# Sampled-token attention in a hybrid decoder layer: cached keys turned together and scored in one visit, cached values in two steps, new tokens' products paired

## The chip, the cores and the metric

The kernel runs on one core of a Trainium2 chip. The metric is device time in microseconds for one execution of the whole layer; lower is better. Three runs of the kernel before took 1364.67, 1366.31 and 1366.91 us, a median of 1366.31.

The engines are named as in the profile: PE (TensorE, matrix products; PEld is its loading of the stationary operand), DVE (VectorE), ACT (ScalarE), POOL (GpSimd) and SP (SyncE, which here only issues DMAs). ACT issues some DMAs as well. Each engine works through its own list in order and waits for others by semaphores.

## The reference, cut to what matters

One layer runs over a prompt (1024 tokens) and over a sample (8 sequences of 4 new tokens, each with cached keys and values). The change touches the sample's dilated attention:

```python
def dilated_attn_cached(q, k, v, buf, d, span):
    # q, k, v: (8, 4, 4 heads, 128); buf: (8, Wb, 2, 4, 128), Wb = 128, 256, 256 for the groups
    kall = concatenate([buf[:, :, 0], k], axis=1)
    vall = concatenate([buf[:, :, 1], v], axis=1)
    idx = Wb + arange(T)[:, None] - arange(span + 1)[None, :] * d
    kg, vg = take(kall, maximum(idx, 0), axis=1), take(vall, maximum(idx, 0), axis=1)
    s = einsum('bthe,btjhe->bthj', q, kg) / sqrt(128)
    s = where(idx >= 0, s, -1e30)
    m = max(s); p = exp(s - m); l = sum(p)
    return einsum('bthj,btjhe->bthe', p, vg) / l, m + log(l)
...
wts = softmax(stack(lses), axis=0)               # over the three groups
o = einsum('gbth,gbthe->bthe', wts, stack(outs))
```

There are three groups, with windows of 128, 512 and 2048 tokens and dilations 1, 4 and 16. The kernel takes one softmax over the scores of all three groups and of the new tokens together, which is the same thing.

## The kernel before

The layer first projects and mixes the recurrent part (to about 640 us). Then come four attention heads (to about 1160 us), the two output branches, the last product and the LayerNorm.

**A head.** Loop `h` runs over 4 heads and inside it `g` over 3 groups. Each (h, g) projects v, k and q: three column blocks of 128, each in two halves of the contraction, each half as 36 products (L178, F32R, 128 by 352): four with the high part of the weights, four with the low part, four with the low part of x, for each of three banks `pj`. A half's weights come by a DMA (`wraw`, SP), are rounded by ACT (`whi`, L168) and the rest is taken by DVE (`wlo`, L169). Three halves' parts are held at a time, two raw ones.

**What runs between.** The attention work of (h, g) is cut into `steps`, which `interleave` (L1247) spreads over the 18 projection slots of the next group: `attend` for the prompt (scores L948, masks L950, exponentials L958, turns L968, products with the values L985), `s_scores` for the sample's scores, and after group 2 also `s_values` (sample's values) and `merge` (the prompt's three groups weighted, with loads `cb` that come back from a small DRAM tensor `cd`). Behind this a scheduler orders each engine's list by its own estimate of durations, so a step's instructions don't always stand where the step does. After head 3 the steps that are left run beside the first 8 slots of the output branch (`branch`, L1308, also with L178).

**The sample's scores.** Per head and group: `cache_keys` (L1027) loads a piece of cached keys (tile `kc`, 2 buffers) so that blocks of 32 by 32 can be turned on DVE (L1056, tile `KT`, 2 buffers); each load is turned in two parts q = 0, 1. `score` (L1059) multiplies four (group 1: two) sequences' queries with one part, each sequence on its own 32-column tile of PE; the results gather in one bank `s`. Group 1 needs two loads (u = 0, 1), the other groups one. `mask` adds the mask and takes maxima, and after group 2 `new` (L1081) multiplies the queries with the new tokens' keys: 24 products of four columns. In steps: turn part 0; score part 0 and turn part 1; and so on; each score is a visit of its own on PE.

**The sample's values.** `turn_new` writes out the new keys and values and puts the new values under group 2's cached ones (tile `c3`); `turn(0)`, `turn(1)` turn the probabilities on PE; `pv0` (group 0's values), `pv1(0)`, `pv1(1)` (two halves of group 1's) and `pv2` (group 2's) add up in banks `o` (sequences 0 to 3) and `s` (4 to 7), by L1147. Each step loads its values itself (`cache`, L1011, tile `kc`); SP issues a load when the buffer that it takes is free. F32 products show as two instructions each in the trace and as one in the lists of order below.

## Time and profile before

| | |
|---|---|
| median of three runs | 1366.31 us |
| profiled execution: time | 1365.17 us |
| profiled execution: first to last instruction (span) | 1363.5 us |
| granted TensorE clock, mean | 0.993 |
| L178 products, the three kinds together | 5544 (projections and first output branch), 1165 us busy |
| sample's scores: L1067 | 192 instructions |
| sample's new tokens: L1086 | 192 instructions |
| sample's cached values: L1147 | 256 instructions |
| HBM traffic | 110.68 MB read, 38.97 MB written |

Times inside the trace count from the span's first instruction. The execution's own time is 1.7 us more than its span, and 1.1 us less than the median of the runs. A line of the timeline gives start, length, engine, line of the program, operation, output and inputs by their names, shapes, how many are merged, and in brackets the idle time before it with what ended it. A matmul's row is longer than the distance to the next one, because they are pipelined; so distances between starts are what a product costs.

### The profile page before, as it was taken

The page shows a single profiled execution, that of the slowest core. Times are in us where ns is not written, and L with a number is a line of the kernel's source. Part 1 is how long each engine was busy: PE and PEld are TensorE (multiplying, and loading weights), DVE is VectorE, ACT ScalarE, POOL GpSimd, SP SyncE. Part 2 cuts the span into 40 slices and gives each one's busy share as a digit, 9 for nine tenths or more (in the row PEclk, how much of TensorE's full clock was granted, in tenths as well). Part 3 has the DMA queues.
Part 4 walks back from the last instruction along what each step waited for, and adds up shares of the span by engine and source line. Part 5 has one row for each costly group of instructions (what it writes and reads, how often), then busy time and mean ns, then how long its engine had stood idle before and what let it go on. Part 6 is the DMA issues. An engine that isn't in the chain of part 4 may idle for free.

```text
span 1363.5 us, 25941 instructions
## 1 busy us (share of the span) xinstructions
PE 1331.7 (98%) x10101; PEld 1241.0 (91%) x10101; DVE 804.4 (59%) x2204; ACT 469.2 (34%) x1065; POOL 67.0 (5%) x82
## 2 busy tenths in 40 slices
PE   9999999999999999999999999999999999999997
PEld 7998999898988999999999999999999998899786
DVE  5677668786476855543554385437543844665565
ACT  5334344434443443422332323232332234132211
POOL 0000000000000000000000000000000000025100
PEclk9999999999999999999999999999999999899999
DMA  6122223122313233328545455555554666795221
GB/s 210 44 61 66 67 86 97 51 75 72 93 61 81 72 109 96 96 89 156 106 109 120 118 132 103 123 129 128 100 120 119 135 130 158 237 286 163 84 100 68
DMA packets 340151, 151.64 MB, mean 111 GB/s; under 512 B 188808, under 2 KB 329502, under 8 KB 339774
## 3 DMA queue, kind: packets, MB, share of 16 engines
q1 hardware_dynamic: 241150, 129.68, 35.0%
q10 hardware_dynamic: 98880, 20.32, 7.5%
q8 instruction: 79, 1.29, 0.4%
q14 instruction: 42, 0.34, 0.1%
HBM read 110.68 MB, written 38.97 MB: 110 GB/s over the span
## 4 chain that ended last, share of the span: by engine, by line
PE 82%; DVE 11%; DMA 3%; issue 1%; SPq 1%; ACT 1%; ACTq 0%; DVEq 0%
PE pj L178 60%; PE pj L1431 7%; PE o L985 2%; PE s L948 2%; DVE tm L457 1%; DVE X L460 1%; PE g L385 1%; PE t L968 1%; PE s L1067 1%; DMA wraw<-in_w_in_dram 1%; PE sc L543 1%; DMA cb<-cd 1%; DVE wlo L169 1%; DVE st L552 1%; PE sc L549 1%
## 5 line engine op out<-in xcount | busy, mean ns | idle before, releaser
L178 PE MATMUL pj<-xhi,whi 128*128 128x352 f32 x1848 | 398.3, 337 | 4.5 <-ACT xhi L1298 3.1
L178 PE MATMUL pj<-xhi,wlo 128*128 128x352 f32 x1848 | 386.1, 330 | 0.0
L178 PE MATMUL pj<-xlo,whi 128*128 128x352 f32 x1848 | 380.5, 327 | 0.0
L178 PEld LDWEIGHTS pj<-xhi,whi 128*128 128x128 f32 x1848 | 304.5, 190 | 20.7 <-issue 10.6
L178 PEld LDWEIGHTS pj<-xlo,whi 128*128 128x128 f32 x1848 | 309.2, 190 | 1.8 <-issue 0.7
L178 PEld LDWEIGHTS pj<-xhi,wlo 128*128 128x128 f32 x1848 | 307.1, 189 | 3.9 <-issue 2.3
L169 DVE TENSOR_TENSOR wlo<-wraw,whi 128x512 fp32r<-128x512 f32 x162 | 112.8, 697 | 89.6 <-ACT whi L168 88.8
L168 ACT ACTIVATE whi<-wraw 128x512 fp32r<-128x512 f32 x162 | 100.5, 625 | 132.5 <-PE pj L178 94.3
L958 ACT ACTIVATE Sm<-Sm,nm 128x128 f32<-128x128 f32 (+1 forms) x96 | 42.4, 442 | 101.8 <-DVE nm L955 101.8
L457 DVE TENSOR_TENSOR tm<-Y,X 128x60 f32<-128x60 f32 (+24 forms) x248 | 52.1, 210 | 10.5 <-DMA Y<-Yd 4.3
L460 DVE TENSOR_TENSOR X<-X,tm 128x60 f32<-128x60 f32 (+24 forms) x248 | 51.9, 209 | 6.0
L552 DVE SCALAR_TENSOR_TENSOR st<-sc,E,SD 64x64 f32<-64x64 f32 x128 | 36.1, 282 | 29.0 <-PE sc L549 27.3
L950 DVE CUSTOM_DVE_ANT_0 Sm<-s,cst 128x128 f32<-128x128 f32 (+1 forms) x96 | 29.2, 347 | 39.6 <-PE s L948 38.9
L1431 PE MATMUL pj<-wl,mh 128*128 128x512 f32 (+1 forms) x136 | 51.9, 382 | 0.0
L541 ACT ACTIVATE SD<-st,E 128x128 f32<-128x128 f32 x64 | 25.6, 401 | 70.5 <-DVE st L552 70.4
L811 POOL TENSOR_TENSOR kvp<-vv,kv 128x512 f32<-128x512 f32 x16 | 20.2, 1262 | 470.8 <-DVE Ss L819 386.7
L985 PE MATMUL o<-PT,Vt 128*128 128x128 f32 x280 | 38.7, 276 | 0.8 <-ACT PT L972 0.8
L948 PE MATMUL s<-k,q 128*128 128x128 f32 (+1 forms) x192 | 37.8, 326 | 1.1 <-DVE ml L950 1.1
L873 ACT ACTIVATE k<-pj 128x352 f32<-128x352 f32 (+1 forms) x36 | 16.2, 455 | 65.1 <-PE pj L178 60.9
L311 ACT ACTIVATE zt<-pj,der 128x352 f32<-128x352 f32 x48 | 26.5, 553 | 33.1 <-PE pj L178 27.8
L985 PEld LDWEIGHTS o<-PT,Vt 128*128 128x128 f32 x280 | 36.4, 191 | 1.5 <-ACT PT L972 1.1
L544 DVE TENSOR_TENSOR W<-sc,R 64x128 f32<-64x128 f32 x64 | 18.4, 288 | 29.5 <-PE sc L543 28.4
(325 smaller groups left out, 1699.4 us busy)
## 6 DMA issues: line engine op xcount, KB each, us to landing
wraw<-in_w_in_dram SPq DMA_DIRECT2D x146, 256.0 KB
gd<-zt SPq DMA_DIRECT2D x48, 176.0 KB
gt<-gd SPq DMA_DIRECT2D x48, 176.0 KB
vs<-bt ACTq DMA_DIRECT2D x48, 128.0 KB
kc<-in_cache_kv_g_dram SPq DMA_DIRECT2D x48, 128.0 KB
Vt<-vs ACTq DMA_DIRECT2D x12, 512.0 KB
cb<-cd SPq DMA_DIRECT2D x12, 512.0 KB
zd<-zt SPq DMA_DIRECT2D x24, 176.0 KB
```

The costliest lines, as they stand in the source:

```text
L168: S.activation(hi[:], raw[:], AF.Copy)
L169: V.tensor_tensor(lo[:], raw[:], hi.bitcast(F32)[:], ALU.subtract)
L178: T.matmul(out, w[wi][:, n % 4, :], x[:, n % 4, :], start=first and n == 0, stop=last and n == 11)
L311: S.activation(t[:], b[:], AF.Tanh, scale=0.5, bias=der[:, HB + col : HB + col + 1])
L457: V.tensor_tensor(tm, Y[:, r : r + 1, r + 1 : 32].to_broadcast([P, m, n]), X[:, 0:m, r : r + 1].to_broadcast([P, m, n]), ALU.mult)
L460: V.tensor_tensor(X[:, 0:m, r + 1 : 32], X[:, 0:m, r + 1 : 32], tm, ALU.subtract)
L552: V.scalar_tensor_tensor(S1[d, d], pS[d, d], E[d, c, 64:65], SD[d, d], ALU.mult, ALU.add)
L948: T.matmul(r, qT[:, i * P : (i + 1) * P], kT[:, keys[i][0] * P : keys[i][0] * P + n], start=True, stop=True)
L950: V.tensor_tensor_reduce(out=Sm[:, i, 0:n], in0=r, in1=m3 if g == 2 else m12[:, 256 - n : 256], scale=1.0, scalar=NEG, op0=ALU.add, op1=AL ...
L958: S.activation(Sm[:, i, 0:n], Sm[:, i, 0:n], AF.Exp, scale=SCALE, bias=nm[:, x : x + 1], accum_out=ml[:, g, 1, i : i + 1])
L985: T.matmul(po[:, (i % 4) * P : (i % 4 + 1) * P], st["Vt"][:, kb_, :], PT[:, n * P : (n + 1) * P], start=m == 0, stop=m == len(keys[i]) - 1,)
L1431: T.matmul(pb[:], a[:, k], wk, start=x == 0, stop=x == len(prods) - 1)
```

## The change

Four things:

- `s_scores`: both parts of a load are turned in two steps of their own, and scored in one (`both`). The number of steps stays (three, for group 1 five).
- `new`: for each group, sequences x and x + 4 (the two that share a column tile) go in one product, eight columns into two runs of four. 24 products become 12.
- `s_values`: the loads of group 0's values and of half 0 of group 1's are issued in `turn(1)`, half 1's at the end of `pv0`. `pv0` also does half 0, `pv2` also half 1: four steps become two.
- the list that mixes `s_values` with `merge` is set anew for six steps in place of eight.

```diff
         def turn(u, q):
             if q == 0:
                 st["c"] = cache_keys(g, h, u)
-            kt = mk(sp, [P, 512], "KT", 2)
+            kt = st["kt", q] = mk(sp, [P, 512], "KT", 2)
             V.transpose(kt[:, 0 : 4 * rows], st["c"][:, 4 * q : 4 * q + 4, :].rearrange("p b n -> p (b n)"))
-            st["kt"] = kt
...
         def new():
             b = ps("s")
-            for bb in range(NB):
-                s_, r = bb // 4, slice(32 * (bb % 4), 32 * (bb % 4) + 32)
-                for gg in range(3):
+            for gg in range(3):
+                for x in range(4):
+                    r = slice(32 * x, 32 * x + 32)
                     T.matmul(
-                        b[r, 12 * s_ + 4 * gg : 12 * s_ + 4 * gg + 4], qS[:, h, gg, :], kS[:, h, gg, 4 * bb : 4 * bb + 4],
+                        b[r, 0:24].rearrange("p (s n) -> p s n", s=2)[:, :, 4 * gg : 4 * gg + 4],
+                        qS[:, h, gg, :], kS[:, h, gg, :].rearrange("p (s b t) -> p b s t", s=2, b=4)[:, x],
                         start=True, stop=True, tile_position=(0, r.start),
                     )
...
-        steps, last = [], None
-        for u in range(2 if g == 1 else 1):
-            for q in range(2):
-                f = (lambda u, q: lambda: turn(u, q))(u, q)
-                steps.append(f if last is None else (lambda a, b: lambda: (a(), b()))(last, f))
-                last = (lambda u, q: lambda: score(u, q))(u, q)
-        steps.append((lambda a: lambda: (a(), mask()))(last))
+        def both(u):
+            score(u, 0)
+            score(u, 1)
+
+        steps = [lambda: turn(0, 0), lambda: turn(0, 1)]
+        if g == 1:
+            steps += [lambda: (both(0), turn(1, 0)), lambda: turn(1, 1), lambda: (both(1), mask())]
+        else:
+            steps += [lambda: (both(0), mask())]
...
         def turn(s_):
             if s_ == 0:
                 st["PT"] = [mk(sp, [P, 512], "KT", 2).rearrange("p (a b) -> p a b", a=4) for _ in range(2)]
+            else:
+                st["c0"], st["c1"] = cache(0, 1, h, 0), cache(1, 1, h, 0)
...
         def pv0():
             st["po"] = [ps("o"), ps("s")]
-            c = cache(0, 1, h, 0)
+            c = st["c0"]
             for bb in range(NB):
                 pv(bb, 0, c[:, bb, :], True, False)
+            pv1(0)
+            st["c1"] = cache(1, 1, h, 1)
 
         def pv1(u):
-            c = cache(1, 1, h, u)
+            c = st["c1"]
...
         def pv2():
+            pv1(1)
             c = st["c3"]
...
-        return [turn_new, lambda: turn(0), lambda: turn(1), pv0, lambda: pv1(0), lambda: pv1(1), pv2, out]
+        return [turn_new, lambda: turn(0), lambda: turn(1), pv0, pv2, out]
...
-                steps += [me[0], sv[1], me[1], sv[2], sv[3], me[2], sv[4], me[3], sv[5], sv[6], me[4], me[5], sv[7]]
+                steps += [me[0], sv[1], me[1], sv[2], me[2], sv[3], me[3], me[4], sv[4], me[5], sv[5]]
```

Three places in the engines' lists show how instructions move. Lines behind the change are counted in the changed file, where L1066, L1085 and L1151 are what L1067, L1086 and L1147 were.

**PE, group 1's first load in head 0** (KT are the turned keys, qS the queries, pj the projections' banks). Lines with a sign differ:

```order
-L1067 MATMUL s_8775<-KT_8737,qS_7812 32x256 x2
 L178 MATMUL pj_8686<-xhi_11_92,whi_8757 128x352 x4
 L178 MATMUL pj_8686<-xhi_11_92,wlo_8758 128x352 x4
 L178 MATMUL pj_8686<-xlo_13_94,whi_8757 128x352 x4
-L968 MATMUL t_8794<-ident_69,Sm_8587 128x128 x4
+L968 MATMUL t_8791<-ident_69,Sm_8587 128x128 x4
 L178 MATMUL pj_8687<-xhi_11_92,whi_8757 128x352 x4
 L178 MATMUL pj_8687<-xhi_11_92,wlo_8758 128x352 x4
 L178 MATMUL pj_8687<-xlo_13_94,whi_8757 128x352 x4
-L1067 MATMUL s_8775<-KT_8778,qS_7812 32x256 x2
+L1066 MATMUL s_8817<-KT_8737,qS_7812 32x256 x2
+L1066 MATMUL s_8817<-KT_8775,qS_7812 32x256 x2
```

The first half's two products moved down by 24 projection products, to stand with the second half's.

**PE, early in head 1**, after the last prompt scores of group 0 (L948), where the half of weights 9721 (in the new list 9709) begins. Before:

```order
L948 MATMUL s_9689<-k_9294,q_9453 128x256 x2
L178 MATMUL pj_9648<-xhi_10_91,whi_9651 128x352 x4
L178 MATMUL pj_9648<-xhi_10_91,wlo_9652 128x352 x4
L178 MATMUL pj_9648<-xlo_12_93,whi_9651 128x352 x4
L1067 MATMUL s_9755<-KT_9716,qS_7812 32x128 x4
L968 MATMUL t_9777<-ident_69,Sm_9566 128x128 x4
L1067 MATMUL s_9755<-KT_9760,qS_7812 32x128
L178 MATMUL pj_9646<-xhi_11_92,whi_9721 128x352 x4
L178 MATMUL pj_9647<-xhi_11_92,whi_9721 128x352 x2
L178 MATMUL pj_9646<-xhi_11_92,wlo_9722 128x352 x4
```

And now:

```order
L948 MATMUL s_9677<-k_9276,q_9440 128x256 x2
L178 MATMUL pj_9636<-xhi_10_91,whi_9639 128x352 x4
L178 MATMUL pj_9636<-xhi_10_91,wlo_9640 128x352 x4
L178 MATMUL pj_9636<-xlo_12_93,whi_9639 128x352 x4
L178 MATMUL pj_9634<-xhi_11_92,whi_9709 128x352 x4
L178 MATMUL pj_9635<-xhi_11_92,whi_9709 128x352 x4
L178 MATMUL pj_9634<-xhi_11_92,wlo_9710 128x352 x4
```

The visit to the sampled keys and the turn L968 left this place (both stand 36 and 48 projection products further down, the keys' eight products together), and eight high products stand ahead of the first low one. Heads 2 and 3 have the same order here.

**PE and SP, the cached values of head 3** (kc are loads of values: in the list of before 13523 is group 0's, 13536 and 13573 the halves of group 1's, in the new one 13466, 13468 and 13521). PE before:

```order
L1147 MATMUL o_13521<-kc_13523,KT_13485 32x128 x4
L1147 MATMUL s_13522<-kc_13523,KT_13486 32x128 x4
L1147 MATMUL o_13521<-kc_13536,KT_13485 32x128 x8
L178 MATMUL pj_13547<-xhi_2217_13178,whi_13278 128x352 x4
L178 MATMUL pj_13547<-xhi_2217_13178,wlo_13279 128x352 x4
L178 MATMUL pj_13547<-xlo_2218_13179,whi_13278 128x352 x4
L1147 MATMUL o_13521<-c_2223_13190,KT_13485 32x128 x4
L178 MATMUL pj_13595<-xhi_2217_13178,whi_13278 128x352 x4
L178 MATMUL pj_13595<-xhi_2217_13178,wlo_13279 128x352 x3
L1147 MATMUL s_13522<-kc_13573,KT_13486 32x128 x4
```

And now:

```order
L1151 MATMUL o_13503<-kc_13466,KT_13437 32x128 x4
L1151 MATMUL s_13504<-kc_13466,KT_13438 32x128 x4
L1151 MATMUL o_13503<-kc_13468,KT_13437 32x128 x8
L178 MATMUL pj_13530<-xhi_2217_13142,whi_13242 128x352 x4
L178 MATMUL pj_13530<-xhi_2217_13142,wlo_13243 128x352 x4
L178 MATMUL pj_13530<-xlo_2218_13143,whi_13242 128x352 x4
L1151 MATMUL o_13503<-c_2223_13154,KT_13437 32x128
L1151 MATMUL s_13504<-kc_13521,KT_13438 32x128 x4
L1151 MATMUL o_13503<-c_2223_13154,KT_13437 32x128 x3
L178 MATMUL pj_13602<-xhi_2217_13142,whi_13242 128x352 x3
L1151 MATMUL s_13504<-kc_13521,KT_13438 32x128 x4
L1151 MATMUL s_13504<-c_2223_13154,KT_13438 32x128 x4
```

Half 1 (13573, now 13521) is used 12 projection products after group 0's values, where it was 19, and its second piece 3 further, where it was 12. In heads 0 to 2 there are 33 such products between, and group 0's values and half 0 share one visit. SP, now:

```order
L1233 DMA cb_13462<-cd_2275_13435 128x1024
L1233 DMA cb_13464<-cd_2275_13435 128x1024
L1327 DMA gt_13615<-gd_371 128x352
L1020 DMA kc_13521<-in_cache_kv_g_dram 128x4x128 x2
L1233 DMA cb_13479<-cd_2275_13435 128x1024
L1233 DMA cb_13526<-zd_95 128x1024
```

Half 1's two pieces stand together behind the first two loads of the merge (cb), in all four heads; before, in heads 0 to 2, they stood ahead of cd, which feeds cb.

More of the change, by code (lines that the diff above doesn't have):

```diff
@@ L1061, in score @@
                 st["b"] = ps("s")
-            kt = st["kt"]
+            kt = st["kt", q]
             nb = 4 * rows // n
```

## The prediction

> **What bounds the kernel now.** I read the page first: busy time by engine, then the chain that ended last.
>
> ```profile
> PE 1331.7 (98%) x10101; PEld 1241.0 (91%) x10101; DVE 804.4 (59%) x2204; ACT 469.2 (34%) x1065; POOL 67.0 (5%) x82
> ...
> PE 82%; DVE 11%; DMA 3%; issue 1%; SPq 1%; ACT 1%; ACTq 0%; DVEq 0%
> ```
>
> TensorE is busy in 98% of the span, and 82% of the chain is its own work. The change touches the attention stage alone (about 640 to 1185 us of the span). There PE hardly ever waits, so time taken out of its stream should come off the end, unless a new wait takes its place. The question for each edit is therefore what one visit to the sampled-token products adds to PE's stream. The timeline tells it.
>
> ```profile
> 672.17 0.81 PE L178 MATMUL pj<-xhi,wlo 128*128 128x352 f32 x4
> 672.82 0.81 PE L178 MATMUL pj<-xlo,whi 128*128 128x352 f32 x4
> 673.55 0.43 PE L1067 MATMUL s<-KT,qS 128*32 128x128 f32 x8
> 673.91 0.91 PE L178 MATMUL pj<-xhi,whi 128*128 128x352 f32 x4
> 674.66 0.33 PE L178 MATMUL pj<-xhi,wlo 128*128 128x352 f32 x1
> ```
>
> Columns: start, length, engine and line, tiles, shapes, count. Four projection products (L178) start 0.65 us apart (672.17 to 672.82). With the visit between them the next four start 1.09 later, 0.44 more, and that group then lasts 0.75 (673.91 to 674.66), 0.10 more. A visit of eight instructions (four products in F32, two each, on four 32-column tiles) costs **0.54 us**. I add the same 0.10 to the visits below.
>
> ```profile
> 774.82 0.81 PE L178 MATMUL pj<-xlo,whi 128*128 128x352 f32 x4
> 775.55 0.65 PE L1147 MATMUL o<-kc,KT 128*32 128x128 f32 x16
> 776.12 0.91 PE L178 MATMUL pj<-xhi,whi 128*128 128x352 f32 x4
> ```
>
> Sixteen of that shape: 1.30 - 0.65 + 0.10 = 0.75. So eight more cost 0.21, and **entering and leaving costs 0.33** whatever is done there.
>
> **The change, part by part.** *Both key halves in one visit.* Per head, group 0 goes from two products' visits to one (head 0), group 1 from four to two, group 2 from two to one.
>
> Group 0, head 0: 2 x 0.54 - 0.75 = 0.33. In heads 1 to 3 the order of before splits it in three (4, 1 and 3 products), so two entries go, and the 0.2 of the product that ran alone: 0.86 each. Sum 0.33 + 3 x 0.86 = **2.9**.
>
> Group 1 holds the largest term, because a half has two products of 256 columns, on two of the four tiles:
>
> ```profile
> 714.65 0.80 PE L178 MATMUL pj<-xlo,whi 128*128 128x352 f32 x4
> 715.38 0.63 PE L1067 MATMUL s<-KT,qS 128*32 128x256 f32 x4
> 715.93 0.92 PE L178 MATMUL pj<-xhi,whi 128*128 128x352 f32 x4
> ```
> ```profile
> 1229.95 0.81 PE L178 MATMUL pj<-al,whi 128*128 128x352 f32 x4
> 1230.68 0.64 PE L1366 MATMUL so<-xt,xhi 128*32 128x256 f32 x8
> 1231.25 0.92 PE L178 MATMUL pj<-ah,whi 128*128 128x352 f32 x4
> ```
>
> Four instructions on two tiles cost 1.28 - 0.65 + 0.10 = 0.73. Eight of the same size on four tiles, as L1366 does for another product, cost 1.30 - 0.65 + 0.10 = 0.75: twice the work for nothing. A merged visit has that shape. Per head 4 x 0.73 - 2 x 0.75 = 1.42; four heads **5.7**. If the tiles did not overlap, only two entries a head would go, 4 x 0.66 = 2.6: that is the low end.
>
> Group 2 loses one entry a head: 4 x 0.33 = **1.3**.
>
> *New tokens' products paired.* 48 instructions become 24, each with eight columns for four:
>
> ```profile
> 759.21 0.81 PE L178 MATMUL pj<-xlo,whi 128*128 128x352 f32 x4
> 759.95 0.98 PE L1086 MATMUL s<-kS,qS 128*32 128x4 f32 x48
> 760.87 0.91 PE L178 MATMUL pj<-xhi,whi 128*128 128x352 f32 x4
> ```
>
> 1.66 - 0.65 + 0.10 = 1.11, so 0.78 beyond the entry, 16 ns each. No row has the new form (output in two runs of four columns). Between nothing saved and the whole 0.78 (24 products as cheap as none, should alternating tiles overlap), I take the half that the count gives, being nearest to this row: 0.39, four heads **1.6**, ends 0 and 3.1. [...]
>
> *Cached values in two steps.* In heads 0 to 2 the new order has four entries where there were five: 3 x 0.33 = **1.0**. What decides here is the last load. Half 1 of group 1's values reuses the buffer of group 0's, so SP issues it only when PE has done the first eight products. In head 3 that was so before, too:
>
> ```profile
> 1174.77 0.49 SPq L1020 DMA_DIRECT2D kc<-in_cache_kv_g_dram  x1
> 1176.71 0.32 SPq L1226 DMA_DIRECT2D cb<-zd  x1
> 1177.08 0.43 SPq L1020 DMA_DIRECT2D kc<-in_cache_kv_g_dram  x1
> ```
> ```profile
> 1179.14 0.43 PE L1147 MATMUL s<-kc,KT 128*32 128x128 f32 x8 [0.19 <-DMA kc<-in_cache_kv_g_dram]
> ...
> 1182.40 0.43 PE L1147 MATMUL s<-kc,KT 128*32 128x128 f32 x8 [0.60 <-DMA kc<-in_cache_kv_g_dram]
> ```
>
> The two pieces landed 4.4 and 5.3 us after issue, and PE waited 0.19 + 0.60. In the new order PE comes to them sooner. The visit of 16 products takes 0.33 + 4 x 0.21 = 1.2, then follow 12 L178 products (1.95) and the entry: 3.2 us from the visit's start, while the issue comes 0.45 into it. With 4.4 to land, PE waits 4.85 - 3.2 = 1.7 (ends 0.8 and 2.6); the second piece, right behind, lands inside the 1.0 that PE then takes. Against 0.8 before, less one entry: head 3 **loses 0.6**.
>
> In heads 0 to 2 there are 33 L178 products between (5.3 us) and a visit of 0.54: 7.1 from the visit's start. But SP now has two 512 KB loads of cb just ahead of this one. How long such a pair takes shows in before:
>
> ```profile
> 776.79 0.81 SPq L1226 DMA_DIRECT2D cb<-cd  x2
> ```
> ```profile
> 783.50 2.02 DVE L1231 TENSOR_TENSOR o<-o,cb 128x1024 f32<-128x1024 f32 x1 [0.62 <-DMA cb<-cd]
> ```
>
> The second, issued at 777.2, let VectorE go at 783.5, after 6.3. Half 1, behind it, lands 6.3 to 7.3 after its own issue, at 6.75 to 7.75, against 7.1: a wait of 0 to 0.65. I take 0.3, three heads: **loses 0.9** (ends 0 and 6, should it take 2 longer).
>
> *What moves at a head's start.* In heads 1 to 3 the sampled keys' visit stood just ahead of a weight half that came barely in time. It moves 48 products down:
>
> ```profile
> 804.11 0.65 PE L178 MATMUL pj<-xlo,whi 128*128 128x352 f32 x3
> ...
> 805.97 1.24 PE L178 MATMUL pj<-xhi,whi 128*128 128x352 f32 x6
> ```
> ```profile
> 804.88 1.14 ACT L168 ACTIVATE whi<-wraw 128x512 fp32r<-128x512 f32 x2
> ```
> ```profile
> 805.27 0.69 DVE L819 TENSOR_TENSOR Ss<-Ss,kvp 128x512 f32<-128x512 f32 x1
> 805.87 0.68 DVE L169 TENSOR_TENSOR wlo<-wraw,whi 128x512 fp32r<-128x512 f32 x1
> ```
>
> PE took the half at 805.97; the high part was done at about 805.5, the low one at 806.55. Without the visit PE is there at 804.11 + 3 x 0.16 = 804.6. The new order puts the high part ahead of two exponentials on ACT, the low part ahead of L819, and eight high products, not six, ahead of the first low one: needed at 804.6 + 8 x 0.16 = 805.9, done at about 805.27 + 0.7 + 0.14 of delay by the second key turn. I take a wait of 0.2, three heads: **loses 0.6** (ends 0, and 2.7 if the high part stays where it was).
>
> *What goes with it.* One wait of before should go:
>
> ```profile
> PE s L948 <- DVE ml L950: 1.1, 1, 1.1
> ```
> ```profile
> 770.68 0.56 DVE L1138 COPY KT<-t 128x384 f32<-128x384 f32 x1 [6.95 <-PE t L1136]
> ```
>
> This copy stood for 6.95 us in front of the merge's last small operations on VectorE, and the load of half 1 in front of its DMA on SP. Both now come after them, so the merge's long multiplications end sooner and no longer hold the next head's first scores: **1.0** back.
>
> **Sum.** 2.9 + 5.7 + 1.3 + 1.6 + 1.0 - 0.6 - 0.9 - 0.6 + 1.0 = 11.4 us, against the profiled execution's 1365.17: 1353.8. That execution lies 1.1 under the median of the three runs (1366.31), from which it would be 1354.9. I forecast **1354.4**.
>
> **The rivals.**
> *No new wait* (0.18). The order lists loads and products where they fit, and the three waits (0.9, 0.6, and head 3's 1.7) may be too long by my rows: 11.4 + 3.2 = 14.6, so 1350.6. Against it: 4.4 us of landing cannot be hidden under 3.2.
> *The tiles do not pair* (0.20). If group 1's second half waits for its first, 3.1 of the 5.7 are lost: 1357.5. L1366 speaks against it, but its products came from one step, and here the second half hangs on a second turn on VectorE.
> *Nothing comes out* (0.06). A wait of the same length at each head's start, where the margin was under 0.5: 1363.6 to 1369.
> *Slower: half 1 of the values comes too late in every head* (0.06). It hangs on PE's own progress, stands behind 1 MB of cb, and SP's later loads stand behind it. Long idling has a second price:
>
> ```profile
> 1160.74 1.25 PE L178 MATMUL pj<-xhi,whi 128*128 128x352 f32 x3 [3.12 <-ACT xhi L1298]
> ...
> 1162.75 1.38 PE L178 MATMUL pj<-xhi,wlo 128*128 128x352 f32 x4
> 1163.93 1.38 PE L178 MATMUL pj<-xlo,whi 128*128 128x352 f32 x4
> ```
>
> After 3.12 us without work four products took 1.18 us, not 0.65; over the 17 to about 1166.8 that is some 2.5 us. [...] A wait of 4 us in each head costs 4 x (4 + 2.5) = 26 for the 14.6 gained: 1377. It decides as soon as the wait reaches 3.1 in every head, that is, from a landing of 9.8 us; the longest seen here is 6.3.
>
> **How the numbers follow.** The forecast has 0.50 and spans about 1352 to 1357 by the ends of the small terms. The range reaches over the two neighbours, 1349.5 to 1360.5, and leaves out the last two cases. About 0.2% (2.7 us) is what a measurement of this kernel can tell from no change. Faster by more: 0.50 + 0.18 + 0.20 = 0.88; within it 0.06; slower 0.06.
>
> **What would show it.** Group 1's visits should have eight instructions and cost 0.75, as L1366's; if they cost 1.2, the tiles do not pair. The new tokens' visit should fall from 1.11 to 0.72. PE should wait for kc under 1 us in heads 0 to 2 and some 1.7 in head 3, and for wlo or whi at the starts of heads 1 to 3 for some 0.2. The wait of L948 should be gone. Wrong would be: L178 products at twice their spacing after a value load, or wlo waits of microseconds at the heads' starts.

## The result, and the profile after

| | before | after |
|---|---|---|
| median of the runs made together (six each) | 1366.61 us | 1354.45 us |
| range of these runs | 1362.72 to 1367.95 us | 1353.07 to 1357.87 us |
| span of the profiled execution | 1363.5 us | 1351.2 us |
| ratio, with its 95% interval | | 0.9918 [0.9898, 0.9937] |

The change takes 12.2 us off the median, and 12.2 off the span. The forecast was 1354.4. The ratio's interval is 5.3 us wide, so the nearness of forecast and median is finer than these runs can tell.

From the page of after: busy time by engine, then the chain that ended last.

```profile
PE 1318.8 (98%) x10005; PEld 1238.6 (92%) x10005; DVE 805.1 (60%) x2204; ACT 469.3 (35%) x1065; POOL 67.6 (5%) x82
PE 82%; DVE 11%; DMA 3%; issue 1%; ACT 1%; SPq 0%; POOL 0%; ACTq 0%; DVEq 0%; POOLq 0%
```

96 instructions fewer on PE (the new tokens' 192 became 96), 13 us less of its time, the same share of the span. PE still bounds the kernel. Group 1's merged visit in head 0, and the new tokens' visit in head 3, from the timeline of after:

```profile
718.67 0.81 PE L178 MATMUL pj<-xlo,whi 128*128 128x352 f32 x4
719.41 0.64 PE L1066 MATMUL s<-KT,qS 128*32 128x256 f32 x8
719.98 0.43 PE L178 MATMUL pj<-xhi,whi 128*128 128x352 f32 x1
```
```profile
1153.48 0.81 PE L178 MATMUL pj<-xlo,whi 128*128 128x352 f32 x4
1154.23 0.38 PE L1085 MATMUL s<-kS,qS 128*32 128x8 f32 x24
1154.53 0.92 PE L178 MATMUL pj<-xhi,whi 128*128 128x352 f32 x4
1155.28 0.81 PE L178 MATMUL pj<-xhi,wlo 128*128 128x352 f32 x4
```

By the prediction's own measure the first is 719.98 - 718.67 - 0.65 + 0.10 = 0.76 (forecast 0.75), the second 1155.28 - 1153.48 - 1.30 = 0.50 (forecast 0.72). At the start of head 1 (PE, ACT and DVE) no wait for weights shows: eight high products, 1.30 us, cover the low part, ready at 802.57 (801.88 + 0.69), 0.12 before it is needed.

```profile
801.39 1.46 PE L178 MATMUL pj<-xhi,whi 128*128 128x352 f32 x8
801.88 0.69 DVE L169 TENSOR_TENSOR wlo<-wraw,whi 128x512 fp32r<-128x512 f32 x1
802.69 0.52 PE L178 MATMUL pj<-xhi,wlo 128*128 128x352 f32 x2
```

The new waits are those for the last load of values (total, count, longest, from the waits of PE):

```profile
PE s L1151 <- DMA kc<-in_cache_kv_g_dram: 3.1, 3, 1.8
PE pj L178 <- ACT xhi L1305: 2.9, 1, 2.9
```

And behind the longest of them, in head 3, the timeline shows something that the sum didn't have, and the windows (start:end, length, then the engines' busy times, and the granted clock as the third number from the end) name it:

```profile
1166.80 0.43 PE L1151 MATMUL s<-kc,KT 128*32 128x128 f32 x8 [1.83 <-DMA kc<-in_cache_kv_g_dram]
...
1169.69 0.94 PE L178 MATMUL pj<-xhi,wlo 128*128 128x352 f32 x2
1170.42 1.38 PE L178 MATMUL pj<-xlo,whi 128*128 128x352 f32 x4
1171.60 1.12 PE L178 MATMUL pj<-xhi,whi 128*128 128x352 f32 x4
```
```profile
1165.20:1168.60 3.40, 1.80 (x33) 1.21 (x33) 3.40 (x3) 0.37 (x1) 0.00 (x0) 1.00 0.86 228
1168.60:1172.00 3.40, 3.40 (x17) 3.30 (x14) 2.41 (x3) 0.53 (x2) 0.00 (x0) 0.54 0.68 217
```

Four products take 1.18 us (1170.42 to 1171.60), not 0.65: some 3.4 us at half clock, which cost 1.7. The other such stretch of after, as long, stands behind the wait of 2.9 for xhi. Before, the clock was halved once in this stage, behind that same wait, but for twice as long: 6.8 us in both, so in the difference of these two executions the half clock cancels.

Both kernels run the same L178 products in the same order, but for 18 that change places at the starts of heads 1 to 3. So the start of the product that has n of them ahead of it, in after less in before, tells where the time went:

| L178 products ahead | what lies behind it | after less before, us |
|---|---|---|
| 2880 | nothing of the change | -0.01 |
| 3096 | head 0, group 0's keys | -0.36 |
| 3312 | group 1's | -1.78 |
| 3460 | group 2's and the new tokens | -2.77 |
| 3540 | head 0's values | -2.99 |
| 3600 | first prompt scores of head 1 | -3.21 |
| 4836 | heads 1 and 2, with their values | -8.96 |
| 4896 | first prompt scores of head 3 | -10.29 |
| 5256 | head 3, group 1's keys | -13.38 |
| 5400 | head 3's values | -12.13 |

Up to head 3's group 1 more came out than the whole sum; head 3's last stage gave 1.25 back.

### The profile page after: what moved, and what is told of

The parts are those of the page before. It is cut to its first block, busy times and chain, and to the rows that moved or that the text cites. A ratio compares the mean times of both kernels' runs of the same rounds, so it can differ in the third digit from the quotient of the medians.

```text
span 1351.2 us, 25749 instructions
## 1 busy us (share of the span) xinstructions
PE 1318.8 (98%) x10005; PEld 1238.6 (92%) x10005; DVE 805.1 (60%) x2204; ACT 469.3 (35%) x1065; POOL 67.6 (5%) x82
## 4 chain that ended last, share of the span: by engine, by line
PE 82%; DVE 11%; DMA 3%; issue 1%; ACT 1%; SPq 0%; POOL 0%; ACTq 0%; DVEq 0%; POOLq 0%
PE pj L178 60%; PE pj L1438 7%; PE s L948 2%; PE o L985 2%; DMA kc<-in_cache_kv_g_dram 2%; DVE tm L457 2%; DVE X L460 2%; PE g L385 1%; PE t L968 1%; DVE st L552 1%; PE sc L543 1%; DVE wlo L169 1%; PE sc L549 1%; DMA cb<-yd 1%; PE sc L528 1%
## 5 line engine op out<-in xcount | busy, mean ns | idle before, releaser
L178 PE MATMUL pj<-xhi,whi 128*128 128x352 f32 x1848 | 396.4, 336 | 4.3 <-ACT xhi L1305 2.9
L178 PE MATMUL pj<-xhi,wlo 128*128 128x352 f32 x1848 | 385.7, 330 | 0.0
L178 PE MATMUL pj<-xlo,whi 128*128 128x352 f32 x1848 | 381.1, 327 | 0.0
L178 PEld LDWEIGHTS pj<-xhi,whi 128*128 128x128 f32 x1848 | 305.3, 190 | 14.4 <-issue 4.4
L178 PEld LDWEIGHTS pj<-xlo,whi 128*128 128x128 f32 x1848 | 309.4, 190 | 2.3 <-issue 1.3
L178 PEld LDWEIGHTS pj<-xhi,wlo 128*128 128x128 f32 x1848 | 307.8, 190 | 3.7 <-issue 1.9
L169 DVE TENSOR_TENSOR wlo<-wraw,whi 128x512 fp32r<-128x512 f32 x162 | 113.9, 704 | 74.4 <-ACT whi L168 73.9
L948 PE MATMUL s<-k,q 128*128 128x128 f32 (+1 forms) x192 | 37.7, 325 | 0.1
L873 ACT ACTIVATE q<-pj 128x352 f32<-128x352 f32 (+1 forms) x36 | 16.4, 455 | 58.4 <-PE pj L178 54.6
```

The costliest lines, as they stand in the source:

```text
L169: V.tensor_tensor(lo[:], raw[:], hi.bitcast(F32)[:], ALU.subtract)
L178: T.matmul(out, w[wi][:, n % 4, :], x[:, n % 4, :], start=first and n == 0, stop=last and n == 11)
L873: S.activation(classes(dst[:], d)[:, :, t0 // d : (t0 + n) // d], b[:, 0:n].rearrange("p (i c) -> p c i", c=d), AF.Copy)
L948: T.matmul(r, qT[:, i * P : (i + 1) * P], kT[:, keys[i][0] * P : keys[i][0] * P + n], start=True, stop=True)
```

## The experiments

Where a time is compared with the kernel before, that kernel ran beside it on the same chip: 1364.76 us for the first four kernels, 1365.34 for the next four, then 1366.19 and 1365.62.

### Each part alone: p1_scores, p2_new, p3_values

On the kernel before, only the hunk of that name in the diff above. Of `s_scores`:

```diff
+        steps = [lambda: turn(0, 0), lambda: turn(0, 1)]
+        if g == 1:
+            steps += [lambda: (both(0), turn(1, 0)), lambda: turn(1, 1), lambda: (both(1), mask())]
+        else:
+            steps += [lambda: (both(0), mask())]
```

> Only the sampled keys' part of the change, on the kernel before. My theory (each visit to PE costs 0.33 us to enter and leave, and group 1's eight instructions on four tiles cost what four on two did): 2.9 + 5.7 + 1.3 = 9.9 us less than before, ratio 0.9928; group 1's visits 0.76 each, eight of them; the new tokens' visit stays at 1.11, and the 1.1 us wait of the prompt's scores L948 on VectorE's masks stays, because the values' part takes that away. Rival 1 (part of the scores' gain needs the values' new order, because the weights' halves come too late at the heads' starts without it): PE waits for wlo or whi there and 7 to 9 us. Rival 2 (the scores' part itself takes the L948 wait away): over 11 us.

of `new`:

```diff
+            for gg in range(3):
+                for x in range(4):
```

> Only the new tokens' products paired, on the kernel before. From the changed kernel's trace, where this visit costs 0.50 us in place of 1.11: 4 x 0.6 = 2.4 us less, ratio 0.998. By the prediction's own term (the count halves, 16 ns an instruction stay): visit 0.72, 1.6 us less. Rival (the visit's cost of 0.50 in the changed kernel comes from its new neighbours, L968 and L985 in one block, not from the pairing): visit 0.9 or more here and under 1 us less. The waits on L948 and on kc stay as before in every theory.

and of `s_values` with its list:

```diff
-        return [turn_new, lambda: turn(0), lambda: turn(1), pv0, lambda: pv1(0), lambda: pv1(1), pv2, out]
+        return [turn_new, lambda: turn(0), lambda: turn(1), pv0, pv2, out]
```

> Only the cached values in two steps with the list of steps set anew, on the kernel before. Theory A, the prediction's terms: one entry a head saved in heads 0 to 2 (1.0 less), waits for half 1 of 0.3 each (0.9 more), head 3 loses 0.6, the L948 wait of 1.1 goes (1.0 less): 0.5 us less than before. Theory B, from the changed kernel's trace: waits for kc of about 0, 0.8, 0.5 and 1.8, and behind the last of them 3.4 us of TensorE at half its clock, which costs 1.7 more: L948 gains 1.8 in all, heads 0 to 2 lose 0.4, head 3 loses 2.6: 1.2 us slower than before. What tells them apart: L178 products 0.29 us apart, not 0.16, for 3.4 us just behind the last values of head 3, and the L948 wait gone in both. Rival C (the L948 wait goes with the scores' part, not with this one): the wait of 1.1 is still there, and 2 to 3 us slower.

| | median | ratio to before | 95% interval |
|---|---|---|---|
| p1_scores | 1358.29 us | 0.9941 | [0.9918, 0.9964] |
| p2_new | 1363.45 us | 0.9982 | [0.9966, 0.9998] |
| p3_values | 1367.10 us | 1.0016 | [1.0000, 1.0032] |

By the ratios 8.1 less (0.9928 was expected, inside the interval), 2.5 less and 2.2 more; by the medians 6.5 and 1.3 less and 2.3 more. The scores' part carries the gain. In p1 group 1's visits cost 0.76, as expected, and PE waits nowhere for weights at the heads' starts, which was rival 1's reason. But in heads 1 to 3 group 0's keys still stand in two visits (ten instructions, then six), so that part gives 0.35, 0.25, 0.29 and 0.29 us here, where after has 0.35, 0.78, 0.72 and 0.73: the rest of that term needs the new list of the values. By the visits p1 saves 1.2 + 6.0 + 1.3 = 8.5 us, in rival 1's range of 7 to 9 and not the theory's 9.9: part of the gain does need the values' new order, but not because of the weights. In p2 the visit costs 0.50 in all four heads, as in after, so its neighbours have no share in it: the rival falls. In p3 PE waits for kc in every head; by the timeline 1.33, 0.12 and 0.91 in heads 0 to 2 and 1.31 in head 3, of which the row of the waits counts the three long ones:

```profile
PE s L1149 <- DMA kc<-in_cache_kv_g_dram: 3.6, 3, 1.3
```

No half clock follows the last, so theory B had the right sign without its second price. L948's wait of 1.1 is missing in p3, but in p1 too, which has the old values: rival 2 of p1, unless that wait goes by itself. r1 below was made for this.

### What the tiles are worth: t1_two_tiles

```diff
-                s_, r = bb // 4, slice(32 * (bb % 4), 32 * (bb % 4) + 32)
+                s_, x = (bb // 2 % 2, 2 * u + bb % 2) if g == 1 else (bb // 4, bb % 4)
+                r = slice(32 * x, 32 * x + 32)
```

> The changed kernel, with group 1's four sequences of one load on two column tiles in place of four (sequences 0 and 2 of a load share one, 1 and 3 another; the second load takes the other two), so that what follows gets its rows in another order and the output is another. Counts and visits stay. Theory (products on different tiles overlap, those on one tile queue): group 1's visits rise from 0.76 to 0.33 + 2 x 0.40 = 1.13, eight visits, so 3.0 us slower than the changed kernel, about 9 us less than before. Rival (the merged visit is cheap because entering and leaving is all that counts, whichever tiles): the visits stay at 0.76 and the time within 0.5 us of the changed kernel.

From its timeline, the visit of head 0 that is shown above for after:

```profile
718.31 0.79 PE L178 MATMUL pj<-xlo,whi 128*128 128x352 f32 x4
719.03 1.06 PE L1067 MATMUL s<-KT,qS 128*32 128x256 f32 x8
720.02 0.59 PE L178 MATMUL pj<-xhi,whi 128*128 128x352 f32 x2
```

The visit costs 720.02 - 718.31 - 0.65 + 0.10 = 1.16, and all eight 1.18 with the next products taken in, 0.42 more than in after; 3.4 us in all (expected 3.0). The median is 1355.59, ratio 0.9924 [0.9899, 0.9949], which the interval does not part from after. The visits decide: **the merged visit is cheap because its second half goes to the two tiles that the first leaves idle**, not only because it enters once.

### Why the new tokens gave more: n1_order and n2_contig

n1, on the kernel before, changes the order alone:

```diff
-            for bb in range(NB):
-                s_, r = bb // 4, slice(32 * (bb % 4), 32 * (bb % 4) + 32)
-                for gg in range(3):
+            for gg in range(3):
+                for bb in range(NB):
+                    s_, r = bb // 4, slice(32 * (bb % 4), 32 * (bb % 4) + 32)
```

> The kernel before, with its 24 unpaired products of new tokens in another order: group by group over the eight sequences, so that neighbours fall on different column tiles, where three in a row had the same one. Nothing is paired. Theory A (the prediction's: 16 ns an instruction, whatever its tile, so that only the count saves): the visit stays at 1.1 us, no change of time. Theory B (what the pairing gained beyond the count, 0.50 in place of the 0.72 forecast, came from the new loop's order, which changes tiles at every product): 0.33 + 48 x 0.007 = 0.67, the 7 ns being the changed kernel's (0.50 - 0.33) / 24; four heads 1.8 us less, ratio 0.9987.

```profile
757.54 0.81 PE L178 MATMUL pj<-xlo,whi 128*128 128x352 f32 x4
758.29 0.58 PE L1086 MATMUL s<-kS,qS 128*32 128x4 f32 x48
758.80 0.59 PE L178 MATMUL pj<-xhi,whi 128*128 128x352 f32 x2
```

The timeline's 48 instructions are all there, and the visit costs 758.80 - 757.54 - 0.65 + 0.10 = 0.71, in all four heads, not 1.11. So of the 0.61 that the pairing saves, 0.40 come from changing the tile at every product and 0.21 from the halved count. Theory B (0.67) holds. The median is 1364.57, ratio 0.9992 [0.9982, 1.0002]: 1.6 us are too few for a time.

n2, on the kernel after, writes the eight columns side by side:

```diff
-                        b[r, 0:24].rearrange("p (s n) -> p s n", s=2)[:, :, 4 * gg : 4 * gg + 4],
+                        b[r, 8 * gg : 8 * gg + 8],
```

> The changed kernel, with each paired product's eight columns written side by side in the bank, not in two runs of four; the columns then stand in another order for what follows, and the sampled rows come out different. Theory (two runs cost nothing): the visit stays at 0.50 and the time within 0.5 us of the changed kernel. [...]

```profile
1158.35 0.80 PE L178 MATMUL pj<-xlo,whi 128*128 128x352 f32 x4
1159.08 0.38 PE L1085 MATMUL s<-kS,qS 128*32 128x8 f32 x24
1159.38 0.91 PE L178 MATMUL pj<-xhi,whi 128*128 128x352 f32 x4
```

In the timeline of n2 the visit costs 1.03 - 0.65 + 0.10 = 0.48, where after has 1.05 between the same rows, so 0.50. Two runs of four columns cost nothing that shows beyond these 0.02. The median is 1356.08, ratio 0.9924 [0.9903, 0.9945], an interval too wide to tell 0.5 us.

### Head 3's wait taken away: v3_own_last, v4_both

```diff
-        c = mk(sp, [P, 8, P], "c3" if last else "kc", 1 if last else 2)
+        c = mk(ap, [P, 8, P], "Vt", 2) if h == 3 and u else mk(sp, [P, 8, P], "c3" if last else "kc", 1 if last else 2)
...
+                if h == 3:
+                    st["c2"] = cache(1, 1, h, 1)
...
-            st["c1"] = cache(1, 1, h, 1)
+            st["c1"] = st["c2"] if h == 3 else cache(1, 1, h, 1)
```

> The changed kernel, with one edit: in head 3 half 1 of group 1's values gets a buffer of its own (one of Vt's, whose last use there is over), so that its load doesn't wait for PE's first values. Heads 0 to 2 as they were. Theory (the late load costs its wait of 1.8 us, and the wait then drops TensorE to half its clock for a window of 3.4 us, another 1.7): no wait for kc or Vt in head 3, no stretch of half clock behind its values, 3.5 us less than the changed kernel, about 1351. Rival 1 (the transfers, not the buffer, are the limit there: the earlier load pushes the loads of cb, gt and the other values back): a wait of 1 us or more at another product of that stage, and under 1.5 us less. Rival 2 (the half clock follows from the wait of 2.9 for ACT's xhi, not from this one): the wait goes, the second stretch of half clock stays, 1.8 us less.

v4 adds:

```diff
-                steps += [me[0], sv[1], me[1], sv[2], me[2], sv[3], me[3], me[4], sv[4], me[5], sv[5]]
+                steps += [me[0], sv[1], me[1], sv[2], me[2], sv[3], me[3], me[4], me[5], sv[4], sv[5]]
```

> As v3_own_last, and in all heads the second step of values stands one step later in the list, which moves it down by 3 to 12 projection products in heads 0 to 2. Theory (waits for kc of 0.8 and 0.5 in heads 1 and 2 come from a load that lands about 0.5 to 0.8 after PE gets there, and everything else there has slack): these waits shrink to 0.3 and less, 0.8 us below v3_own_last, about 1350 and 4 below the changed kernel. Rival (the later step delays the next head's first stage by its loads): PE waits for wlo or whi, or on L948, at the heads' starts, and it is no faster than v3_own_last.

v3: median 1353.03, ratio 0.9914 [0.9900, 0.9927]. v4: 1353.40, 0.9920 [0.9908, 0.9933]. Neither can be told from after (0.9918). In v3 the wait is gone, and so is the half clock (the window that shows 0.54 in after, in v3's windows):

```profile
1168.60:1172.00 3.40, 3.40 (x23) 3.40 (x23) 3.40 (x5) 0.18 (x1) 0.00 (x0) 1.00 0.69 196
```

Between the L178 products with 5256 and 5400 ahead of them, v3 takes 2.5 us less than after. But up to the one with 5543 ahead, 1.8 come back, in two waits that after doesn't have (waits of PE in v3):

```profile
PE pj L178 <- DVE xhi L1335: 1.5, 1, 1.5
...
PE pj L178 <- DVE xlo L1335: 1.0, 1, 1.0
```

L1335 is the output branch's product on VectorE, which empties a bank pj. Rival 2 falls, since the half clock went with the wait. Theory and rival 1 each had a part: the wait and its half clock cost 2.5, but of the 3.5 less that was expected only 0.7 is left. The loads did move, as rival 1 has it: in v3 the first two loads of cb go out at 1160.59, in after at 1157.99, and VectorE starts the merge's first addition at 1168.98, in after at 1167.03.

In v4 the waits for kc in heads 0 to 2 sum to 1.2, against 1.93 in v3, but v5 and v6 below, with v3's order there, have 1.43 and 1.37, and 1.1 of v4's is one wait, in head 1, where 0.3 or less was expected. So the later step isn't shown to help. Behind head 3 v4 has the same two waits (0.9 and 1.3).

### What holds that stage: v5_pool_add, v6_pool_merge

v5 moves the merge's additions in head 3 off VectorE, v6 all of its head 3 merge:

```diff
-                V.tensor_tensor(yv, yv, oc, ALU.add)
+                (G if h == 3 else V).tensor_tensor(yv, yv, oc, ALU.add)
```

> As v3_own_last, and in head 3 the merge's two additions of 128x1024 run on GpSimd, not on VectorE. Theory (v3 took 2.4 us out of head 3's values, and 1.8 came back because PE's projection products then waited 1.5 and 1.0 us for VectorE's products at L1335, which free their banks and stand behind the merge's long operations): the wait of 1.5 goes or falls under 0.5, 1 to 1.5 us less than v3_own_last, if GpSimd's addition, which takes an estimated 2.7 us by 1.33 for half that size (L811), does not make the merge's end late. Rival (the later loads, not VectorE, set the end of that stage): the sum of PE's waits behind head 3's values stays at 2 to 3 us and the time as in v3_own_last.

```diff
+        E = G if h == 3 else V
...
-            V.tensor_tensor(oc, oc, nat, ALU.mult)
+            E.tensor_tensor(oc, oc, nat, ALU.mult)
...
-                V.tensor_tensor(yv, yv, oc, ALU.add)
+                E.tensor_tensor(yv, yv, oc, ALU.add)
...
-            V.tensor_tensor(y[:], y[:], cb[3][:], ALU.mult)
+            E.tensor_tensor(y[:], y[:], cb[3][:], ALU.mult)
```

> As v3_own_last, and the whole merge of head 3 (three products, two additions, the last product, each 128x1024) runs on GpSimd. In v3 and v5 the last of them ends VectorE's part at about 1176, as in the changed kernel, and the products of the output branch (L1335 there) that free PE's banks stand behind it. Theory (that queue behind the merge, not the transfers, took back what head 3's values gave): with VectorE free of it PE's wait for xhi of 1.5 goes, and the wait for xlo of 1.0 with it if it follows from the same delay: 1.5 to 2.5 us less than v3_own_last. GpSimd, at the 2.9 us that v5 shows for an addition, ends the merge some 5 us later, with the loads that need it far from used. Rival (the loads of gt hold the branch): the sum of PE's waits there stays over 2 us. Rival 2 (the merge's later end delays the second branch's input): a new wait of PE behind 1195, slower than v3_own_last.

v5: median 1353.38, 0.9902 [0.9885, 0.9920]. The waits there are 2.26 and 0.44, 2.7 together: the rival's numbers, but they don't show its cause. The 2.26 is for a product of VectorE at 1175.95 that stands behind the merge's last product (L1246, at 1174.82), and this one needs GpSimd's addition (to 1174.35). Beside that addition an operation of VectorE that takes 0.71 in v3 took 3.30:

```profile
1171.60 3.30 DVE L169 TENSOR_TENSOR wlo<-wraw,whi 128x512 fp32r<-128x512 f32 x1
```

v6: 1360.41, 0.9965 [0.9949, 0.9980], seven slower than v3. Its profiled execution (1356.86) is the fastest of eight, so its trace shows only about four of the seven. The timeline of v6, GpSimd, SP, VectorE and PE in turn (SP's rows are issues; L1247 is the merge's last product, L1248 its store, L1330 the loads of gt for the branch):

```profile
1177.05 2.40 POOL L1247 TENSOR_TENSOR o<-o,cb 128x1024 f32<-128x1024 f32 x1
```
```profile
1179.47 0.32 SPq L1248 DMA_DIRECT2D yd<-o  x1
1179.88 1.23 SPq L1330 DMA_DIRECT2D gt<-gd  x2
```
```profile
1183.43 0.52 DVE L1336 SCALAR_TENSOR_TENSOR xlo<-gt,pj 128x352 f32<-128x352 f32 x1 [3.44 <-DMA gt<-gd]
```
```profile
1184.00 1.54 PE L178 MATMUL pj<-xhi,whi 128*128 128x352 f32 x4 [4.08 <-DVE xlo L1336]
```

The merge ends at 1179.45, its store goes out on SP, two loads of gt right behind it, VectorE waits 3.44 for them, PE 4.08 for VectorE; a second wait, of 1.80, follows. In v3 the same store went out at 1176.54, 2.9 earlier; VectorE waited 2.18 for gt behind it, and PE not at all there:

```profile
1176.54 0.32 SPq L1247 DMA_DIRECT2D yd<-o  x1
1177.57 0.82 SPq L1329 DMA_DIRECT2D gt<-gd  x2
```
```profile
1181.20 0.95 DVE L1335 SCALAR_TENSOR_TENSOR xlo<-gt,pj 128x352 f32<-128x352 f32 x2 [2.18 <-DMA gt<-gd]
```

So rival 1 of v6 has the sum (5.9) and, for the 4.08, the cause; rival 2 has "slower", but not its reason, as PE waits nowhere behind 1195. The two waits of v3 are others. Its 1.5 is for a product that stands on VectorE behind the merge's second addition:

```profile
1173.01 1.95 DVE L1243 TENSOR_TENSOR o<-o,o 128x1024 f32<-128x1024 f32 x1
1174.84 0.54 DVE L1335 SCALAR_TENSOR_TENSOR xhi<-gt,pj 128x352 f32<-128x352 f32 x1
```

That is the theory of v5 and v6, and with the merge off VectorE, in v6, this wait is gone. In after the same product stands ahead of that addition (1172.04, the addition at 1172.47). The 1.0 of v3 is for a product that stands on VectorE behind `al`, the split of the second branch's input, which waits for ACT's `ah`:

```profile
1185.32 1.23 DVE L1308 TENSOR_TENSOR al<-xt,ah 128x1024 fp32r<-128x1024 f32 x1 [3.16 <-ACT ah L1307]
...
1187.91 0.51 DVE L1335 SCALAR_TENSOR_TENSOR xlo<-gt,pj 128x352 f32<-128x352 f32 x1
```

And `ah` waits 5.96 us for loads of what the merge's store wrote. So the merge holds that stage in two ways, by VectorE's list and by its store with what stands or hangs behind it, and v6 took away the first at the price of the second. No run took away both. In after the store goes out at 1176.25, PE was 2.5 us later there, and its wait for the values cost most of what it would otherwise have waited behind the merge.

### The values left alone, and the kernel before once more: s1_no_values, r1_before_again

s1 is the kernel before with the hunks of p1 and p2. r1 is the kernel before, with no edit.

> The kernel before with the sampled keys' part and the new tokens' pairing, the values as they were (four steps, the old list). Theory A (the values' part gives nothing: one entry of 0.33 saved in each of heads 0 to 2, against waits for half 1 that sum to 1.3 to 2.4 us over these heads in the kernels with the new order and are 0 in those with the old one; head 3's waits for values are alike in both, 0.8 to 3.9 in the old order and 1.3 to 3.0 in the new one): within 1 us of the changed kernel, 1353.5 to 1355.5, no wait for kc in heads 0 to 2, the wait of L852 (0.3 to 0.9 us) there. Theory B (the prediction's: the values' part is worth 0.5 us by itself, and together with the others it takes a wait of L948 of 1.1 away): 0.5 to 1.5 slower than the changed kernel, with L948's wait there.

> The kernel before, unchanged, profiled once more. Theory (two terms of the sum rested on waits that come and go from one execution to the next): the wait of L948 of 1.1 us at the start of head 3, which was missing also in kernels that left the values alone, may be elsewhere or nowhere, and head 3's wait for kc, 0.8 in the first profile, lies anywhere from 0.8 to 3.9. Rival (they belong to the kernel before): 1.1 at L948 at the same place and 0.8 for kc, to 0.2 us.

s1: median 1355.48, ratio 0.9912 [0.9895, 0.9929]: 1.0 above after by the medians, 0.0006 below it by the ratios. The values' part is worth nothing that these times can tell. Theory A had the time, but its trace has a wait of L948 of 1.0 (at the start of head 2), as B wanted. And as in p1, group 0's keys stand in two visits in heads 1 to 3 of s1 (1.19 with L968, and 0.54), so by the visits the new list is worth 0.4 to 0.5 in each of them, some 1.3 in all, which neither theory had; against it stand the waits for kc in the table below.

r1: one time, 1364.49, span 1362.8. At the start of head 3 the timeline of before has the first of these rows, that of r1 the second, the same products without a wait:

```profile
1066.10 1.13 PE L948 MATMUL s<-k,q 128*128 128x256 f32 x4 [1.10 <-DVE ml L950]
```
```profile
1065.06 1.13 PE L948 MATMUL s<-k,q 128*128 128x256 f32 x4
```

and its waits for kc in head 3 are 1.57 and 0.92:

```profile
1178.13 0.43 PE L1147 MATMUL s<-kc,KT 128*32 128x128 f32 x8 [1.57 <-DMA kc<-in_cache_kv_g_dram]
...
1181.72 0.43 PE L1147 MATMUL s<-kc,KT 128*32 128x128 f32 x8 [0.92 <-DMA kc<-in_cache_kv_g_dram]
```

The same program: 1.1 for L948 became 0.1, 0.8 for kc became 2.5. Waits of PE, summed from the timelines of all profiled executions (us):

| execution | order of the values | kc, heads 0 to 2 | kc, head 3 | L948 at heads' starts | L852 | half clock, 1140 to 1195 |
|---|---|---|---|---|---|---|
| before | old | 0 | 0.79 | 1.10 | 0.62 | 6.8 |
| r1 | old | 0 | 2.49 | 0.10 | 0.57 | 3.4 |
| p1 | old | 0 | 1.90 | 0 | 0.62 | 3.4 |
| p2 | old | 0 | 1.96 | 1.21 | 0.90 | 10.2 |
| n1 | old | 0 | 3.89 | 0 | 0.27 | 6.8 |
| s1 | old | 0 | 1.36 | 1.01 | 0.67 | 6.8 |
| after | new | 1.27 | 1.83 | 0 | 0 | 6.8 |
| p3 | new | 2.37 | 1.31 | 0 | 0 | 6.8 |
| t1 | new | 1.78 | 3.04 | 0 | 0 | 6.8 |
| n2 | new | 1.39 | 2.42 | 0 | 0 | 6.8 |
| v3, v5, v6 | new, own buffer in head 3 | 1.93, 1.43, 1.37 | 0 | 0 | 0 | 3.4, 6.8, 10.2 |
| v4 | as v3, second step later | 1.2 | 0 | 0 | 0 | 6.8 |

In head 3 the mean is 2.07 in the old order (six) and 2.15 in the new one (four), over ranges of 0.8 to 3.9 and 1.3 to 3.0: no loss shows there. In heads 0 to 2 the new order waits 1.65 (mean of seven, without v4) where the old one never waits. L948 waits 1.0 or more in three of six executions of the old order and in none of the new; L852 (the sampled recurrence's transposes, waiting for VectorE) 0.3 to 0.9 in all six and in none of the new.

## Why the prediction was right, point by point

The time was right to 0.1 us by the medians, the range and the sign as well. That nearness is luck in two ways: the sum, 11.4, was 0.7 short of what came out, and 1354.4 was taken between the two times that the sum gave from two bases, 1353.8 and 1354.9. The terms, with what they measured by the table of L178 starts and the visits (in the order of the sum, us less than before):

| term | forecast | measured |
|---|---|---|
| group 0's keys, with the heads' starts | 2.9 - 0.6 | 0.35 + 0.78 + 0.72 + 0.73 = 2.6 |
| group 1's keys | 5.7 | 1.42 + 1.56 + 1.50, and 1.52 for head 3 (from p1): 6.0 |
| group 2's keys | 1.3 | 0.31, 0.35, 0.31 in heads 0 to 2: 1.3 for four |
| new tokens | 1.6 | 4 x 0.61 = 2.4 |
| values, heads 0 to 2 | 1.0 - 0.9 | 0.26 - 0.60 - 0.30 = -0.6 |
| L948 | 1.0 | 1.1 in this pair of executions |
| L852 | not in the sum | 0.6 |
| the rest: head 3's last stage, and the first prompt scores of heads 1 to 3 | -0.6 | 12.1 - 13.4 = -1.3 |
| sum | 11.4 | 12.1 |

The rest is what is left over, not measured term by term; in it the first prompt scores of heads 1 to 3 take 0.2 to 0.3 us less each, beside L948's wait, and the cause of that is open.

*The entry and the tiles.* The sum's main idea held: 0.33 for entering (group 2, which saves nothing else, gave 0.31 to 0.35 a head), and group 1's merged visit at the price of L1366's. Group 0's visits of sixteen instructions cost 0.76 (0.75 forecast), group 1's of eight 0.76 (0.75). So the tiles do pair, against that rival, and t1 shows that the saving comes from them.

*Heads' starts.* The forecast wait of 0.2 for the low part is not there. The weights were early enough behind eight high products (0.12 us in head 1), and the whole gain of group 0 stayed.

*New tokens.* The count was the wrong cause for most of it. "I take the half that the count gives": 0.39 a head; the count gives 0.21 (n1's 0.71 to 0.50), the change of tile 0.40. The row of 16 ns an instruction was that of six instructions in a row on one tile; the same 48, alternating, cost 8 in n1. The new form's output in two runs of four columns, for which the prediction had no row, costs nothing that shows: 0.50 in after, 0.48 side by side in n2.

*Values, heads 0 to 2.* Forecast +0.1, measured -0.6; the waits were mis-sized, 0.9 forecast against 1.27 here and 1.65 on the mean. Half 1's load was late, as forecast, and stands behind two loads of cb on SP; that these two make it late wasn't tried.

*Head 3.* The 1.7 us were nearly met (1.83), and the step "against 0.8 before" failed: 0.8 was the shortest of six executions of the old order, whose mean is 2.07, so the row that set it came from one lucky execution. Two things stand beside it: the half clock of 1.7 behind the wait, which the prediction kept for waits of 3.1 (L178 products at twice their spacing behind a value load were its own sign of being wrong, and here they are), and the merge, which would have stopped PE for most of that time anyway (v3).

*L948.* The 1.0 came, but r1 shows that the wait was largely gone without any change. The values' order may still keep it away (none of 1.0 in the new order, three of six in the old): on the mean of the old order it is worth 0.6, and as much for L852, which the sum didn't have and which separates the orders in every execution. That a copy's long standing on VectorE was its cause wasn't tried.

*The rivals.* "No new wait" fell, as kc waited 3.1 us in after; "nothing comes out" and "slower" as well. Of the latter one half was there: a half clock behind a value wait, at 1.8 us, once, not in every head.

So the forecast's nearness is in part chance: the new tokens gave 0.8 more and L852 0.6, the values and the rest took 1.4 more. And the change's worth, as far as times show it, is in the keys and the new tokens: s1 has those alone and isn't slower than after by any interval here. What the values' new list gives by the traces (some 1.3 in group 0's visits, 0.6 each for L852 and perhaps L948) and what it takes (0.6 in heads 0 to 2) is too little for these times.

## What to carry to other kernels

In these runs small products on column tiles of PE cost by how they alternate (the new tokens' 48 instructions 1.11 us in runs of six on one tile, 0.71 with the tile changed at every product; group 1's eight 1.16 us on two tiles, 0.76 on four): put products for different tiles next to each other, and finish a visit's tiles together, before counting instructions. Before a wait is taken out of a stage, look for what comes behind it: here VectorE's list behind the merge, and the loads of what the merge's store wrote, stopped PE instead, so 2.5 us gained became 0.7. And a wait that hangs on a transfer is read from several executions: one program showed 0.8 and 2.5 us for the same wait, so a loss or gain of 1 us that is read off one trace may have the wrong sign.

## What the runs showed of the hardware

- In after two stretches of half clock (granted 0.50) lie between 1140 and 1195 us, of 3.4 us each, in before one of 6.8; four L178 products took 1.18 us there, not 0.65. One of after's stands behind a wait much shorter than the 3.12 us of the prediction: 1.83. But 2.42 in n2 (1169.82 to 1172.24) brought none, as these windows show: PE works for 1.02 us in the first, and has its full clock in both.

```profile
1168.80:1172.20 3.40, 1.02 (x7) 0.53 (x5) 3.27 (x3) 0.00 (x0) 0.00 (x0) 1.00 0.99 312
1172.20:1175.60 3.40, 3.36 (x43) 2.71 (x44) 2.88 (x4) 0.73 (x2) 0.00 (x0) 1.00 0.84 235
```

  So a wait's length alone doesn't tell whether half clock follows; what does wasn't shown. Two executions of one program differ by 1.7 us in this: behind the wait for xhi, 3.12 in before and 2.9 in r1, the half clock lasted 6.8 us and 3.4.
- Twenty-four small products on alternating tiles cost 7 ns each beyond the entry, (0.50 - 0.33) / 24; 48 in runs of six on one tile cost 16, (1.11 - 0.33) / 48; the same 48 alternating 8, (0.71 - 0.33) / 48.
- In v5 and v6 an operation of VectorE, L169, took longer beside GpSimd's work on the merge: 3.30 us in v5 and 2.47 in v6, 0.71 in v3.
